# Expert layers: the layer norm's output added on VectorE and transposed onto the accumulators, in place of 32 products with the identity

## The chip, the cores and the metric

The kernel runs on one core of one Trainium2 chip. The metric is the time of one launch in microseconds (us), as the median of the runs. The engines of the core are named as the profile names them: PE is TensorE (PEld its weight loads, PEq and PEldq its queue), DVE is VectorE, ACT is ScalarE, POOL is GpSimd and SP is SyncE, which here starts the loads of the weights.

## What is computed

The reference takes 256 tokens of width 1024 through two blocks. The first has a feed-forward part, a mixer of attention and a recurrence, and a second feed-forward part. The second block has two layers, and each of them ends in the stage of this change: a layer norm, a mixture of 16 experts, and a term `ple` with a gate, summed before another layer norm.

```python
for i in range(DEPTH_2):
    ...
    x = layer_norm(DEEPNORM_ALPHA * x + mix, ln_mix_g[i], ln_mix_b[i])
    ple = (p[i] @ ple_w_proj[i]) * jax.nn.sigmoid(x @ ple_w_gate[i])
    ffn = grouped_moe(x, router_w, router_bias, moe_w1[i], moe_w3[i], moe_w2[i])
    x = layer_norm(DEEPNORM_ALPHA * x + ffn + ple, ln_ffn_g[i], ln_ffn_b[i])
```

`grouped_moe` picks two experts of a group for every token, and each expert computes `(silu(x @ w1) * (x @ w3)) @ w2`, weighted with the token's gate. The `x` on the last line is the layer norm's output itself; the change is about how this one summand comes into the sum.

## The kernel before

`moe_layer` emits one of the two expert layers. Eight pairs of experts, p = 0 to 7, run one after another in the loop at line 1397. The tokens that chose an expert are gathered into at most CAP slots by a product with one-hot columns (`gather`, tiles `xgp` in PSUM and `xg` in SBUF; `onehot` makes the columns `oh` on DVE). For each pair PE computes `h1` and `h3` (`up`, in the profile both called `h`), ACT and DVE make `es` of them (`hidden`), PE transposes it to `ehT` (`hidden_T`, line 1347), and `down` gives `ey`, two PSUM tiles for the two halves of the columns. ACT and DVE split `ey` into a rounded part `yh` and the rest `yl` (lines 332 and 335), and `combine` spreads both back over the tokens with the transposed one-hot columns `ohT`.

The loop is staggered. In the turn of pair p, PE starts `h1` of pair p + 1, transposes `es` of pair p, and goes on with `h1`; after `ey` of pair p comes `h3` of pair p + 1. I write h1(5) for the h1 of pair 5 and so on.

Up to pair 2, `combine` adds into SBUF tiles `acc` (the kernel's `x[t]`, one per half t of the tokens), since the gate's product holds the four PSUM accumulators. From pair 3 on, which is `last`, the accumulators are `comb`, two tiles of 512 columns for each half of the tokens, and the products add into them directly. At p == 3 the gated term `pg` is added onto `acc` on DVE (line 1424), and 32 products with the identity add the layer norm's output to `comb`: it lies transposed in SBUF as `xTh` (rounded) and `xTl` (the rest), eight chunks of 128 columns each, and a product with `identr` transposes a chunk back while it adds it. At p == 6 `acc` is split once more and added to `comb`, by 8 products with the identity.

```python
1437            if p == last:
1438                for t in range(2):
1439                    tk = slice(t * P, (t + 1) * P)
1440                    for k in range(8):
1441                        for t_ in (xTh, xTl):
1442                            mm(comb[t][k // 4][:, k % 4 * P:(k % 4 + 1) * P], t_[k][:, tk], identr,
1443                               start=False, stop=False, skip_group_check=True)
```

`mm` (line 342) is the helper that issues most products, so they bear line 343 in the profile.

At the start of p == 4, each engine loads `ci`, the largest number of tokens of an expert (line 1399), and branches on it (line 1400): if it exceeds CAP, `overflow` computes the surplus tokens, on all engines. With the inputs here the branch skips this code. On each engine some instructions of the turn of pair 3 come ahead of this branch and some behind it.

What sets the order: the code is written in the order of the source, and a scheduler then reorders each engine's instructions within a stretch without a branch, by the dependences and its own costs. The tiles come from pools with few slots, taken in turn: `Q` (SBUF, 512 columns, 9 slots), `PT` (PSUM, 4 slots), `PA` (PSUM, 4 slots, which the accumulators hold). A tile that takes the slot of an earlier one waits until that one has been read for the last time. SP streams the weights into rings of slots in SBUF.

## Time and profile before

| what | value |
|---|---|
| median of 3 runs | 1340.25 us (1339.31 to 1346.04) |
| span of the profiled execution, first to last instruction | 1338.8 us |
| PE busy | 1278.3 us, 95% of the span |
| DVE busy | 616.8 us, 46% |
| ACT busy | 521.4 us, 39% |
| expert layers' branch | at 794 us (first layer) and 1210 us (second) |

The profiled execution has no time of its own apart from its span, which lies 1.45 us below the median of the runs; what stands around the span, the launch and its end, is in that difference. The views used below are these. The timeline lists the work of an engine in order, with start and duration in us and, in brackets, the idle time ahead of it and what ended that; a row with "x16" holds 16 instructions in a row, and the duration of a product goes to the end of its last result, which overlaps with the start of the next row. A matmul of type f32 with 512 columns appears as two instructions. A view of a line lists the instructions of one source line, with the queue's own (TENSOR_LOAD, COMPARE_BRANCH, EVENT_SEMAPHORE) among them. Windows give the busy time of each engine in a stretch and PEclk, the granted clock of TensorE as a share of full speed.

### The profile page before, as it was taken

Reading aid. Unit: us, or ns where it says so; the run is one execution under the profiler, and the core shown is the slowest. Engines: PE = TensorE matmul, PEld = TensorE weight load, DVE = VectorE, ACT = ScalarE, POOL = GpSimd, SP = SyncE. Lnnn points to the kernel's source line nnn. Section 1 sums busy time; section 2 is a strip of 40 time slices with the busy share of each in tenths; the row PEclk is TensorE's granted clock in tenths of the full one; section 3 lists DMA queues with packets and bytes.
Section 4 is the critical chain, followed back from the end, with each engine's and each line's share of the span. In section 5 each row is a group of like instructions: output and inputs, shape, how many; then the busy total and the mean of one; then the engine's idle time right before and its main releaser. Section 6 shows DMA issues by size and latency. Waiting matters only on the chain. (4 is left out here: it accounts for less than half of the span.)

```text
span 1338.8 us, 19707 instructions
## 1 busy us (share of the span) xinstructions
PE 1278.3 (95%) x7758; PEld 908.3 (68%) x7758; DVE 616.8 (46%) x1021; ACT 521.4 (39%) x806; POOL 225.8 (17%) x224
## 2 busy tenths in 40 slices
PE   8999999999889999989999999997999999999996
PEld 7999997877879999878544554334988635454432
DVE  6544458796956476485341221107555522131113
ACT  5444445575445554335321131104686421131110
POOL 4000010002484263230011020004021110220001
PEclk9999999999999999999999999997999999998998
DMA  9766656444356556649899989998536698999990
GB/s 338 221 188 189 189 157 198 133 155 144 111 157 190 158 160 199 201 162 311 294 343 362 396 319 377 389 381 282 189 104 206 226 385 318 380 342 356 377 399 34
DMA packets 175277, 335.41 MB, mean 251 GB/s; under 512 B 10337, under 2 KB 72305, under 8 KB 175170
## 3 DMA queue, kind: packets, MB, share of 16 engines
q1 hardware_dynamic: 173696, 330.34, 71.2%
q0 software_dynamic: 896, 2.98, 0.6%
q8 instruction: 66, 1.08, 0.3%
q10 hardware_dynamic: 578, 0.67, 0.1%
q14 instruction: 41, 0.34, 0.1%
HBM read 332.91 MB, written 1.05 MB: 249 GB/s over the span
## 5 line engine op out<-in xcount | busy, mean ns | idle before, releaser
L316 DVE TENSOR_TENSOR wlo<-w,whi 128x1024 fp32r<-128x1024 f32 x200 | 254.5, 1278 | 201.7 <-ACT whi L301 197.8
L301 ACT ACTIVATE whi<-w 128x1024 fp32r<-128x1024 f32 x234 | 246.2, 1059 | 254.9 <-PE hT L339 107.2
L343 PE MATMUL h<-w,xg 128*64 128x512 f32 x1024 | 253.9, 606 | 0.0
L338 PE MATMUL hT<-xTh,whi 128*128 128x256 f32 x704 | 201.4, 286 | 3.1 <-ACT whi L301 3.0
L340 PE MATMUL hT<-xTh,wlo 128*128 128x256 f32 x704 | 200.5, 285 | 1.4 <-DVE wlo L316 1.4
L339 PE MATMUL hT<-xTl,whi 128*128 128x256 f32 x704 | 200.5, 285 | 0.2
L343 PEld LDWEIGHTS h<-w,xg 128*64 128x64 f32 x1024 | 73.3, 138 | 137.4 <-issue 128.1
L338 PEld LDWEIGHTS hT<-xTh,whi 128*128 128x128 f32 x704 | 136.5, 194 | 4.8 <-ACT whi L301 3.4
L340 PEld LDWEIGHTS hT<-xTh,wlo 128*128 128x128 f32 x704 | 136.2, 194 | 2.1 <-DVE wlo L316 2.0
L339 PEld LDWEIGHTS hT<-xTl,whi 128*128 128x128 f32 x704 | 136.2, 194 | 1.3 <-DVE xTl L334 0.8
L343 PE MATMUL ey<-w,ehTs 128*64 128x512 f32 x512 | 115.1, 595 | 0.2
L343 PEld LDWEIGHTS ey<-w,ehTs 128*64 128x64 f32 x512 | 38.3, 137 | 65.1 <-issue 60.8
L335 DVE SCALAR_TENSOR_TENSOR yl<-ey,sgate,yh 128x512 fp32r<-128x512 f32 x32 | 23.6, 749 | 124.2 <-ACT yh L332 123.4
L316 POOL TENSOR_TENSOR wlo<-w,whi 128x1024 fp32r<-128x1024 f32 x16 | 38.0, 2397 | 238.4 <-ACT whi L301 204.7
L338 PE MATMUL tr<-xTh,whi 128*128 128x256 f32 x256 | 73.6, 288 | 0.4 <-ACT xTh L332 0.4
L339 PE MATMUL tr<-xTl,whi 128*128 128x256 f32 x256 | 73.4, 287 | 0.3 <-DVE xTl L334 0.3
L340 PE MATMUL tr<-xTh,wlo 128*128 128x256 f32 x256 | 72.7, 284 | 0.4 <-DVE wlo L316 0.4
L339 PE MATMUL yacc<-wlo,hh 128*128 128x512 f32 x176 | 68.8, 391 | 2.0 <-DVE wlo L316 2.0
L1341 DVE TENSOR_TENSOR es<-es,h 128x512 f32<-128x512 f32 x16 | 11.0, 686 | 129.6 <-PE h L343 103.0
L338 PE MATMUL yacc<-whi,hh 128*128 128x512 f32 x176 | 68.8, 391 | 0.0
L340 PE MATMUL yacc<-whi,hl 128*128 128x512 f32 x176 | 68.6, 390 | 0.0
L332 ACT ACTIVATE yh<-ey,sgate 128x512 fp32r<-128x512 f32 x32 | 21.6, 687 | 113.8 <-PE ey L343 113.4
(444 smaller groups left out, 2142.7 us busy)
## 6 DMA issues: line engine op xcount, KB each, us to landing
w<-in_moe_w SPq DMA_DIRECT2D x384, 512.0 KB, 8.4
w<-in_ffn_w SPq DMA_DIRECT2D x132, 512.0 KB, 4.5
w<-in_w_in SPq DMA_DIRECT2D x28, 512.0 KB, 4.2
w<-in_sb_qkv SPq DMA_DIRECT2D x24, 512.0 KB, 10.3
w<-in_ple_gate SPq DMA_DIRECT2D x16, 512.0 KB, 8.0
w<-in_w_out SPq DMA_DIRECT2D x8, 512.0 KB, 3.4
w<-in_ab_w_in SPq DMA_DIRECT2D x8, 512.0 KB, 4.8
w<-in_ab_w_out SPq DMA_DIRECT2D x8, 512.0 KB, 3.6
```

The lines of the kernel that those rows point to most:

```text
L301: a = S.activation(hi, t, AF.Copy)
L316: i = eng.tensor_tensor(lo, t, fb(hi), op=OP.subtract)
L332: cur["act"] = S.activation(hi, src, AF.Copy if isinstance(scale, float) else AF.Identity, scale=scale)
L335: return V.scalar_tensor_tensor(lo, src, scale, fb(hi), op0=OP.mult, op1=OP.subtract)
L338: PE.matmul(o, lh, rh, start=start, stop=False)
L339: PE.matmul(o, lh, rl, start=False, stop=False)
L340: PE.matmul(o, ll, rh, start=False, stop=stop)
L343: PE.matmul(o, l, r, start=start, stop=stop, **kw)
L1341: V.tensor_tensor(s, s, h3, op=OP.mult)
```

## The change

The function that makes the transposed output now hands out the whole tiles too. At p == 3, after `combine`, four DVE adds sum the rounded part and the rest from SBUF into tiles `yT`, 16 PE transposes turn these into four PSUM tiles `yn`, and four DVE adds of 128x512 add `yn` onto `acc`. The identity products onto `comb` are gone; the 8 at p == 6, which add `acc`, are as before and now bring the layer norm's output too. Comments and some blank lines are also removed. The diff, cut to this:

```diff
@@ layer_norm_T: later
             split(0)
             split(1)
-            return chunks()
+            return chunks(), (hi, lo)
@@ moe_layer
             if p == 0:
-                xTh, xTl = xT()
+                (xTh, xTl), (whole_h, whole_l) = xT()
@@ moe_layer
             combine(p, y, o)
             if p == last:
+
+                yT = [Q([2, T], name="yT") for _ in range(4)]
+                for n in range(4):
+                    c = slice(n % 2 * 2, n % 2 * 2 + 2)
+                    V.tensor_tensor(yT[n], fb(whole_h[n // 2])[:, c], fb(whole_l[n // 2])[:, c], op=OP.add)
                 for t in range(2):
-                    tk = slice(t * P, (t + 1) * P)
-                    for k in range(8):
-                        for t_ in (xTh, xTl):
-                            mm(comb[t][k // 4][:, k % 4 * P:(k % 4 + 1) * P], t_[k][:, tk], identr,
-                               start=False, stop=False, skip_group_check=True)
+                    for kk in range(2):
+                        pn = PT([4, P], name="yn")
+                        for k in range(4):
+                            PE.transpose(pn[:, k, :], yT[2 * kk + k // 2][:, k % 2, t * P:(t + 1) * P], ident)
+                        d = slice(kk * 512, (kk + 1) * 512)
+                        V.tensor_tensor(x[t][:, d], x[t][:, d], pn.rearrange("p a b -> p (a b)"), op=OP.add)
             if p == 6:
```

Added lines shift the numbers of the lines behind; the branch keeps its lines 1399 and 1400.

The scheduler gives another order around the branch. On PE, in the first layer (the second is alike), this piece of the difference is the place right ahead of the branch; `comb` first twice for the first half of the tokens:

```order
 L343 MATMUL comb<-yh,ohT 128x512 x2
 L343 MATMUL comb<-yl,ohT 128x512 x2
+L343 MATMUL comb<-yh,ohT 128x512 x2
+L343 MATMUL comb<-yl,ohT 128x512 x2
+L1447 MATMUL yn<-identr,yT 128x128 x16
 L1399 TENSOR_LOAD ci
 L1400 COMPARE_AND_BRANCH
```

The four `comb` products of the second half and all 16 transposes now stand ahead of PE's load of `ci`. Behind the branch, at the place where its two paths meet, the difference is this (`h_9737` is h1(5)):

```order
 L1400 UNCONDITIONAL_BRANCH x2
-L343 MATMUL comb<-yh,ohT 128x512 x2
-L343 MATMUL comb<-yl,ohT 128x512 x2
-L343 MATMUL comb<-identr,xTh 128x128
-L343 MATMUL comb<-identr,xTl 128x128
...
 L343 MATMUL h_9737<-w_7530,xg 64x512
```

The four `comb` products and the 32 identity products are gone from here, and h1(5) follows the branch directly.

On DVE, ahead of the branch in the first layer, before (waits name the engine whose semaphore is awaited; `es_7705` is es of pair 4, `ci_6743` the count):

```order
L1424 TENSOR_TENSOR acc_7070<-acc_7070,pg_7660 128x512 [waits DVE_49]
L1424 TENSOR_TENSOR acc_7070<-acc_7070,pg_7664 128x512 [waits DVE_49]
L1341 TENSOR_TENSOR es_7705<-es_7705,h3_7672 128x512 [waits PE_49,Activation_49]
L1399 TENSOR_LOAD ci_6743 [waits DVE_49]
L1400 COMPARE_AND_BRANCH
```

and in the changed kernel:

```order
L1424 TENSOR_TENSOR acc_7070<-acc_7070,pg_7664 128x512 [waits DVE_49]
L1442 TENSOR_TENSOR yT_7716<-xTh_6982,xTl_6984 128x512 [waits DVE_49]
L1442 TENSOR_TENSOR yT_7717<-xTh_6982,xTl_6984 128x512 [waits DVE_49]
L1341 TENSOR_TENSOR es_7705<-es_7705,h3_7672 128x512 [waits PE_49,Activation_49]
L1442 TENSOR_TENSOR yT_7718<-xTh_6983,xTl_6985 128x512 [waits PE_49]
L1442 TENSOR_TENSOR yT_7719<-xTh_6983,xTl_6985 128x512 [waits PE_49]
L1449 TENSOR_TENSOR acc_7069<-acc_7069,yn_7724 128x512 [waits PE_49]
L1449 TENSOR_TENSOR acc_7069<-acc_7069,yn_7730 128x512 [waits PE_49]
L1449 TENSOR_TENSOR acc_7070<-acc_7070,yn_7736 128x512 [waits PE_49]
L1449 TENSOR_TENSOR acc_7070<-acc_7070,yn_7742 128x512 [waits PE_49]
L1399 TENSOR_LOAD ci_6743 [waits DVE_49]
L1400 COMPARE_AND_BRANCH
```

All eight adds stand ahead of the branch. `yT_7718` and `yT_7719` wait for PE: their slots are those of `yh` of pair 3, which `comb` of the second half reads last. The adds onto `acc` wait for the transposes. `yT_7716` and `yT_7717` stand ahead of `es`.

The third place is PE behind `ey` of pair 4, in the first layer; before (`h3_9829` is h3(5), `yh_9821` the first half of the columns of pair 4):

```order
L343 MATMUL ey_9788<-w323_7673,ehTs_9759 64x512
L343 MATMUL h3_9829<-w324_7675,xg_7444 64x512 [waits DMAHW2_49,DVE_49,Activation_49]
L343 MATMUL h3_9829<-w325_7681,xg_7444 64x512 [waits DMAHW3_49]
L343 MATMUL h3_9829<-w324_7675,xg_7444 64x512
L343 MATMUL h3_9829<-w325_7681,xg_7444 64x512
L343 MATMUL comb_7668<-yh_9821,ohT_9782 128x512 [waits Activation_49]
L343 MATMUL xgp_9870<-oh_9865,nh_6560 128x256 [waits DVE_49,PE_49]
```

and in the changed kernel:

```order
L343 MATMUL ey_9788<-w323_7673,ehTs_9759 64x512
L343 MATMUL comb_7668<-yh_9821,ohT_9782 128x512 [waits Activation_49]
L343 MATMUL comb_7670<-yh_9821,ohT_9782 128x512
L343 MATMUL h3_9829<-w324_7675,xg_7444 64x512 [waits DMAHW2_49,DVE_49,PE_49]
L343 MATMUL comb_7669<-yh_9823,ohT_9782 128x512 [waits Activation_49]
L343 MATMUL comb_7668<-yl_9822,ohT_9782 128x512 [waits DVE_49]
L343 MATMUL xgp_9870<-oh_9865,nh_6560 128x256 [waits DVE_49,PE_49]
```

`comb` on `yh` of pair 4 now follows `ey` directly, where four products of h3(5) stood between them. Further on, between the last product of h3(5) and the transposes of `es` of pair 5, there stood seven `comb` products and four of h1(6); now there are one of each.

## Rows read from the trace of the kernel before

**Rows 1.** The page: span, and busy time (share of the span) of the engines.

```profile
span 1338.8 us, 19707 instructions
...
PE 1278.3 (95%) x7758; PEld 908.3 (68%) x7758; DVE 616.8 (46%) x1021; ACT 521.4 (39%) x806; POOL 225.8 (17%) x224
```

**Rows 2.** Chain of work that ended last, first work behind the second branch: start us, us, what.

```profile
1213.36 7.37 PE comb L343 x36
```

**Rows 3.** Waits of PE, 1213 to 1330 us: us in total, times, longest us.

```profile
PE comb L343 <- PEq L1400: 2.0, 1, 2.0
PE comb L343 <- ACT yh L332: 1.6, 2, 0.8
PE ehT L1347 <- DVE es L1341: 0.9, 1, 0.9
```

**Rows 4.** Timeline of PE around the first branch: start us, us, engine, line, operation.

```profile
794.42 0.73 PE L343 MATMUL comb<-yh,ohT 128*128 128x512 f32 x2
...
797.70 0.70 PE L343 MATMUL comb<-yh,ohT 128*128 128x512 f32 x2 [2.08 <-PEq L1400]
...
798.81 0.31 PE L343 MATMUL comb<-identr,xTh 128*128 128x128 f32 x1
...
805.66 5.18 PE L343 MATMUL h<-w,xg 128*64 128x512 f32 x16
810.77 0.66 PE L1347 MATMUL ehT<-identr,es 128*128 128x128 f32 x4
811.36 3.65 PE L343 MATMUL h<-w,xg 128*64 128x512 f32 x16
```

**Rows 5.** Timeline of PE around the second branch.

```profile
1210.20 0.73 PE L343 MATMUL comb<-yh,ohT 128*128 128x512 f32 x2
...
1214.36 0.22 PE L343 MATMUL comb<-identr,xTh 128*128 128x128 f32 x1
...
1220.66 5.89 PE L343 MATMUL h<-w,xg 128*64 128x512 f32 x16
1226.48 0.66 PE L1347 MATMUL ehT<-identr,es 128*128 128x128 f32 x4
```

**Rows 6.** Line 1399, the load of ci: ns min/median/max, first and last start us.

```profile
L1399 PEldq TENSOR_LOAD <-ci x2: 315/400/485, 790.9 to 1206.7; - x2
```

**Rows 7.** Line 1400, the branch, in the queues of PE and DVE, same columns.

```profile
L1400 PEldq COMPARE_BRANCH  x2: 6032/6060/6087, 791.5 to 1207.1; - x2
L1400 DVEq COMPARE_BRANCH  x2: 72/72/72, 795.3 to 1210.9; - x2
...
L1400 DVEq EVENT_SEMAPHORE  x2: 21/21/21, 801.0 to 1211.4; - x2
```

**Rows 8.** Line 343, semaphore instructions in PE's queue.

```profile
L343 PEldq EVENT_SEMAPHORE  x68: 51/51/51, 412.2 to 1316.2; - x68
```

**Rows 9.** Line 1424, the adds of the gate onto the accumulators.

```profile
L1424 DVE TENSOR_TENSOR acc<-acc,pg x8: 684/686/689, 787.4 to 1206.2; 128x512 f32<-128x512 f32 x8
```

**Rows 10.** Timeline of PE at an earlier pause, in the mixer.

```profile
600.03 1.19 PE L343 MATMUL pool<-wsum,poolw 128*128 128x256 f32 x2 [4.07 <-DVE yg L994]
```

**Rows 11.** A window of 2 us behind the second branch: busy times, PEclk, DMA, GB/s.

```profile
1216.00:1218.00 2.00, 2.00 (x12) 2.00 (x11) 0.93 (x1) 0.00 (x0) 0.00 (x0) 0.50 1.05 386
```

**Rows 12.** Windows of 1 us after the earlier pause, same columns.

```profile
603.00:604.00 1.00, 1.00 (x4) 0.72 (x3) 0.81 (x2) 0.97 (x4) 0.00 (x0) 0.51 1.01 287
604.00:605.00 1.00, 1.00 (x6) 0.83 (x5) 0.42 (x1) 0.07 (x1) 0.00 (x0) 1.00 0.95 358
```

**Rows 13.** Timeline of PE behind ey of pair 4, first layer.

```profile
822.58 1.89 PE L343 MATMUL h<-w,xg 128*64 128x512 f32 x8
824.40 0.50 PE L343 MATMUL comb<-yh,ohT 128*128 128x512 f32 x1
```

**Rows 14.** Waits of PE's weight loads on a DMA, 797 to 912 us.

```profile
PEld h L343 <- DMA w<-in_moe_w: 0.9, 3, 0.4
```

**Rows 15.** Timeline of DVE behind ey of pair 4, first layer.

```profile
824.21 0.75 DVE L1168 TENSOR_TENSOR oh<-cst,rank 128x256 fp32r<-128x256 f32 x2
```

## Prediction

> **What bounds the kernel now.** I read the page first: PE is busy for 95% of the span, DVE for 46% [rows 1]. Then the chain that ended last: in the second expert layer it enters at the branch, its first piece of work is the 36 products that the change touches, and from there it is PE with few exceptions to the end [rows 2]. The waits of PE in that stretch show the exceptions: 2.0 us at the branch, 1.6 us for yh (two times), 0.9 us for es [rows 3]. No transfer is among them; even the weight loads, which run ahead, waited for a DMA 0.9 us in the largest group of the first expert layer [rows 14]. So a microsecond that PE loses or gains behind the branch should reach the end, in both layers. The place to cost is the stretch around the branch, in the timeline of PE [rows 4, 5].

> I call the start of the first comb product of pair 3 zero: 794.42 in the first layer, 1210.20 in the second. Before, h1(5), the first projection of pair 5, starts at +11.24 (805.66) and +10.46 (1220.66), and ehT(4), the transposes of pair 4, at +16.35 (810.77) and +16.28 (1226.48) [rows 4, 5]. The term for each layer is how these two move.

> **What goes.** The 32 identity products lie back to back on PE: 798.81 to 805.66 is 6.85 us in the first layer, 1214.36 to 1220.66 is 6.30 us in the second [rows 4, 5], 13.15 us together. [...] Ahead of it PE had stood idle for 2.08 us at the branch [rows 4].

> **What comes on VectorE.** Eight adds of 128x512 per layer. The nearest rows, eight adds of the same size, take 684 to 689 ns [rows 9]: 5.5 us, some 0.65 us from start to start when they follow each other. The two for yT0 and yT1 fit into the time in which DVE waits for h3; the other six don't. The order shows why: yT2 and yT3 take the slots of yh and so wait for comb of the second half of the tokens, and the four adds onto acc wait for the transposes.

> **What comes on PE, and what moves.** 16 transposes of 128x128. The four of ehT take 810.77 to 811.36, 0.59 us [rows 4], so 16 take 2.4 us at the high clock. The important thing is where they stand. Before, comb of the second half and the identity products stand behind the branch; now comb of the second half and the transposes stand ahead of it, and behind it stands h1(5) at once. So nothing is left that PE can do between the branch and h1(5).

> **The branch.** PE's sequencer spends 6.03 to 6.09 us in the compare-and-branch [rows 7]; with the load of ci ahead of it, from 790.9 [rows 6] to 797.70 [rows 4] is 6.8 us. Most of this is hidden before: the sequencer came to ci 3.5 us ahead of the first comb product (790.9 against 794.42), while PE still had queued products to run, and PE stood idle for 2.08 us only. After, the sequencer must first issue transposes that wait for DVE. That it stands still at such a wait is what I infer from a semaphore instruction of its queue: the last one is at 1316.2 [rows 8], just where the 0.9 us wait for es in [rows 3] ends, not ahead of it. So I take it that ci is reached only when yT3 is done.

> That moment, from zero: four comb products take 1.1 us (797.70 to 798.81 [rows 4]), eight 2.2 to 2.3. The yh products of the second half are the fifth and the sixth; they end at about +1.5 and +1.85 and set yT2 and yT3 free, which at 0.69 us each end at +2.2 and +2.9. I allow 0.3 us for the rest of the issue: ci at +3.2, 6.35 us or so later than before, and the first product behind the branch at 3.2 + 6.7 = **+9.9**.

> The second bound for h1(5) is DVE, for h1(5) also waits until DVE has passed the branch. Its last add onto acc starts at about +4.85, after 4 x 0.65 us from +2.9; ci and the branch end at +5.5. How long the passage takes, the trace tells two ways: in the first layer the semaphore behind the branch is at 801.0, 5.7 us after the branch at 795.3; in the second at 1211.4, 0.5 us after 1210.9 [rows 7]. I take each layer as it was: **+11.25** in the first, +6.0 in the second. The later of PE and DVE decides: h1(5) starts at +11.25 and +9.9.

> The rows thus show passages of some 6 us (PE twice, DVE once) and of 0.5 us (DVE once) [rows 7], and nothing in the trace binds the kind to the layer. [...]

> **The clock after the longer pause.** The transposes end at about +4.45, so PE now stands idle for 5.4 to 6.8 us, against 2.08. The nearest row with a long pause is 600.03: PE resumed after 4.07 us idle [rows 10] and the clock stayed low to 604.0, then rose to 1.00 [rows 12]. At half speed 3.97 us do the work of 1.99. The first half of h1(5), 16 products, is the size of the second half, 3.65 us at the high clock with the last product's tail [rows 4], some 3.55 without; so 3.55 + 2.0 = 5.55 us to ehT. Bounds: 3.55 (all high) and 7.1 (all low); the rows of before, 5.18 and 5.89 [rows 4, 5], lie between. ehT(4) starts at 11.25 + 5.55 = +16.8 in the first layer, +0.45 against before, and at 9.9 + 5.55 = +15.45 in the second, -0.8.

> **What moves behind ey(4).** Before, four products of h3(5) stand between ey(4) and comb of pair 4, 822.58 to 824.40 or 1.8 us, and cover the making of yh; PE has no idle time there [rows 13]. Now comb stands directly behind ey. Where PE waits for yh elsewhere, it is 0.8 us each time [rows 3]; I take 0.8, bounds 0 and 0.8. The gather xgp needs the one-hot columns, which DVE makes behind yl: 824.21 to 824.96 [rows 15], 1.6 to 2.4 us behind ey's end at 822.58, the first of them at 2.0. With yh 0.7 us later, that is 2.7; ahead of xgp now stand four comb products and one of h3, 1.1 + 0.45 us, behind the wait of 0.8, so PE comes there at about 2.3 and waits 0.4 (bounds 0 and 0.7). Between h3(5) and ehT(5) one comb and one h1 product are left, 0.7 us; es takes 0.9 us where nothing covers it [rows 3], so 0.2 remain (0 to 0.4). Sum +1.4 per layer (0 to 1.9), +2.8 in all. The comb products that no longer cover ehT(5) are not lost; they do their work earlier.

> **The sum.** +0.45 - 0.8 + 2.8 = +2.45 us. The profiled execution's span is 1338.8 [rows 1], 1.45 below the median of 1340.25; I add to the median: **1342.7 us**. 13.15 us of products go and nearly all of it comes back, as idle time at the branch (about 4 us more in each layer), as transposes and as uncovered waits. The runs of before reach from 1339.31 to 1346.04, and 0.5%, 6.7 us, is about what a measurement of this kernel can tell from no change.

> **The rivals.**
> 1. *The forecast, but DVE passes quickly in the first layer too.* Then h1(5) starts at +9.9 there as well: 1.35 us less, 1341.4. For it: DVE passed in 0.5 us in the second layer [rows 7]. Against: 5.7 us in this one.
> 2. *PE's sequencer runs ahead past the waiting transposes.* For it: it was 3.5 us ahead before. Against: [rows 8]. Then ci is reached at about zero, the branch ends at +6.7, and ehT starts at 6.7 + 5.55 = about +12.3 where DVE is quick: -4.0 in each layer, with +2.8 behind: 1335.0; with DVE slow in the first layer, +0.45 there, 1339.5.
> 3. *The plain gain.* The products go, and nothing takes their place: 1340.25 - 13.15 = 1327.1. Against: the order; no work of PE stands between the branch and h1(5).
> 4. *Slower, by DVE at the branch.* DVE takes 5.7 us in both layers, PE stands idle for 6.8 us, and the clock stays low through all of the first half of h1(5): ehT at 11.25 + 7.1 = +18.35, 2.0 and 2.1 later than before, and the waits behind ey at their upper ends, 2 x 1.9: +2.0 + 2.1 + 3.8 = +7.9, 1348.2. It decides as soon as the passage of DVE in the second layer exceeds 4.4 us (9.9 - 5.5). For it: 5.7 us in the first layer. Against: 0.5 us in the second.
> 5. *The change doesn't do what it says.* The order excludes it: the identity products are gone.

> **How the numbers follow.** Forecast 0.45, rival 1 0.22, rival 2 0.14, rival 3 0.04, rival 4 0.15. Predicted is the likeliest, 1342.7. Faster by over 0.5% (below 1333.5): rival 3 and a little of rival 2, 0.06. Slower by over 0.5% (above 1347): most of rival 4, 0.12. The rest, 0.82, is within. The range leaves out rival 3, a part of rival 2 and the upper half of rival 4: 1335 to 1348.

> **What would show it.** In the profile of the changed kernel: the load of ci on PE behind the start of comb, at about +3.2; PE's idle time ahead of h1(5) 5 to 7 us, put down to the branch; a granted clock of 0.50 for some us after it; the semaphore of DVE behind the branch 5.7 or 0.5 us after it; waits of comb for yh at pair 4. The forecast is wrong if PE's pause stays near 2 us (rival 2), if the clock is full at once (about 2 us less per layer), or if a wait on a DMA appears behind the branch, which would mean that the stream of weights, and not PE, sets the pace there.

## The result, and the profile after

The changed kernel is slower: a median of 1351.17 us (1347.02 to 1352.79) against 1341.15 us of before on the same chip, ratio 1.0055 with a 95% interval of [1.004, 1.007], which is +7.4 us (5.4 to 9.4). I had forecast 1342.7 us (+2.45 on the median of before), between 1335 and 1348. The sign of the sum was right and its size was not, and the time lies outside the range. The medians are 10.0 us apart, but a median of so few runs jumps, since the runs of before alone reach from 1339.31 to 1346.80; the ratio is worked out from all runs. Differences below go by the ratio unless the text names the medians or the timelines.

The page of after: the span, and busy time of the engines (share of the span), to be laid beside [rows 1].

```profile
span 1349.4 us, 19658 instructions
...
PE 1277.1 (95%) x7726; PEld 902.8 (67%) x7726; DVE 625.1 (46%) x1037; ACT 520.5 (39%) x806; POOL 226.1 (17%) x224
```

32 identity products per layer are gone, yet PE's busy time falls by 1.2 us only, and the span is 10.6 us longer. The waits of PE from 785 us to the end, after (us in total, times, longest us):

```profile
PE h L343 <- PEq L1400: 12.0, 2, 6.1
PE comb L343 <- ACT yh L332: 5.6, 7, 0.8
```

The lines of the same view of before that stand against these:

```profile
PE comb L343 <- PEq L1400: 4.0, 2, 2.1
PE comb L343 <- ACT yh L332: 3.2, 4, 0.8
```

The wait at the branch has tripled, and it is now `h` that waits, not `comb`. The wait for yh has grown too. The timeline of PE around the two branches, after (start us, us, engine, line, operation, count, idle time ahead and what ended it):

```profile
797.84 0.73 PE L343 MATMUL comb<-yh,ohT 128*128 128x512 f32 x2
...
799.79 2.17 PE L1447 MATMUL yn<-identr,yT 128*128 128x128 f32 x16
808.09 5.29 PE L343 MATMUL h<-w,xg 128*64 128x512 f32 x10 [6.12 <-PEq L1400]
813.63 1.93 PE L343 MATMUL h<-w,xg 128*64 128x512 f32 x6 [0.25 <-issue]
815.49 0.66 PE L1347 MATMUL ehT<-identr,es 128*128 128x128 f32 x4
...
1218.01 0.73 PE L343 MATMUL comb<-yh,ohT 128*128 128x512 f32 x2
...
1219.96 2.17 PE L1447 MATMUL yn<-identr,yT 128*128 128x128 f32 x16
1227.97 6.14 PE L343 MATMUL h<-w,xg 128*64 128x512 f32 x16 [5.84 <-PEq L1400]
1234.04 0.66 PE L1347 MATMUL ehT<-identr,es 128*128 128x128 f32 x4
...
1238.93 7.14 PE L343 MATMUL ey<-w,ehTs 128*64 128x512 f32 x32
1246.83 0.73 PE L343 MATMUL comb<-yh,ohT 128*128 128x512 f32 x2 [0.76 <-DMA w<-in_moe_w]
```

Zero, the first comb product of pair 3, is now 797.84 and 1218.01. From it h1(5) starts at +10.25 and +9.96 and ehT(4) at +17.65 and +16.03. Before, ehT(4) stood at +16.35 and +16.28 [rows 4, 5], so the stretch around the branch costs 1.30 us in the first layer and gains 0.25 in the second. The rest is lost behind it. From ehT(4) to the first comb product of pair 4 is 12.79 us in the second layer of after (1234.04 to 1246.83).

In numbers, from the timelines of both kernels: from ehT(4) to the end of ey(4) 12.03 us (before 11.81) in either layer; from there to the first comb product of pair 5, 36.85 and 36.86 us (before 33.97 both times). That is 0.22 + 2.88 = 3.10 us per layer. (For before, the end of ey(4) is where h3(5) starts beside its last results, 822.58.) With the border, 1.30 - 0.25 + 2 x 3.10 = 7.25 us, which is the +7.4 of the ratio. The profiled execution lost 3.4 us more, all ahead of the first instruction that the change touches: zero of the first layer lies at 797.84 against 794.42, with the same instructions before it. Single executions differ by that much: in the traces of all the kernels here zero of the first layer lies between 792.54 (e6) and 798.75 (e4). So I leave it out, and compare kernels below also by the timelines, from zero to the first comb product of pair 7, both layers together. That stretch is 230.6 us in before and 237.9 in after.

The queues at the branch in after: PE's load of ci, then the branch on PE and DVE and the semaphore of DVE behind it (ns min/median/max, first and last start us), to be laid beside [rows 6, 7].

```profile
L1399 PEldq TENSOR_LOAD <-ci x2: 315/405/495, 800.7 to 1220.9; - x2
...
L1400 PEldq COMPARE_BRANCH  x2: 6209/6250/6292, 801.3 to 1221.3; - x2
L1400 DVEq COMPARE_BRANCH  x2: 72/72/72, 802.6 to 1222.6; - x2
L1400 DVEq EVENT_SEMAPHORE  x2: 21/21/21, 803.9 to 1223.2; - x2
```

PE reaches ci at +2.86 and +2.89, where before it was there 3.5 us ahead of zero. It spends 6.2 to 6.3 us in the branch. DVE passes in 1.3 and 0.6 us, quickly in both layers. The granted clock (PEclk, the number behind the five engines' busy times) in 1 us windows of after:

```profile
812.00:813.00 1.00, 1.00 (x2) 0.00 (x0) 0.00 (x0) 0.00 (x0) 0.00 (x0) 0.50 0.35 109
...
814.00:815.00 1.00, 1.00 (x6) 0.27 (x2) 0.00 (x0) 0.00 (x0) 0.00 (x0) 1.00 0.96 360
...
1232.00:1233.00 1.00, 1.00 (x4) 0.26 (x2) 0.00 (x0) 0.00 (x0) 0.00 (x0) 0.50 0.61 109
1233.00:1234.00 1.00, 1.00 (x6) 0.15 (x2) 0.00 (x0) 0.00 (x0) 0.00 (x0) 0.99 0.61 201
```

After the pause of 6 us PE works at a granted clock of 0.50, the level of [rows 11], for about 5 us (808.09 to 813, 1227.97 to 1233), longer than the 3.97 us of [rows 12].

Behind ey(4), first layer, after, the rows in which PE waits or goes on with h3(5):

```profile
828.28 0.74 PE L343 MATMUL comb<-yh,ohT 128*128 128x512 f32 x2 [0.76 <-ACT yh L332]
828.95 1.07 PE L343 MATMUL h<-w,xg 128*64 128x512 f32 x2
829.95 0.50 PE L343 MATMUL comb<-yh,ohT 128*128 128x512 f32 x1
...
830.96 1.93 PE L343 MATMUL h<-w,xg 128*64 128x512 f32 x6
832.82 0.39 PE L343 MATMUL xgp<-oh,nh 128*128 128x256 f32 x1
...
856.47 7.09 PE L343 MATMUL ey<-w,ehTs 128*64 128x512 f32 x32
864.37 0.73 PE L343 MATMUL comb<-yh,ohT 128*128 128x512 f32 x2 [0.81 <-ACT yh L332]
```

Here is what the forecast had not seen. Products of `h` and `ey` have tiles of 64 columns (128*64), and the records show two of them running side by side: each appears as two rows, and 8 rows, four products, take 1.82 us from start to start in [rows 13] (822.58 to 824.40). A group of one product (x2) and a group of three (x6) together hold the same four, but take 1.00 us (828.95 to 829.95) and 1.86 (830.96 to 832.82), 2.86 in all. A product without a partner, here, took as long as two. I call a group boundary after an odd number of products a torn pair. There are five of these between ey(4) and ey(5) in each layer of after. Before had three, and one more that drew in ey(5). The timeline of PE of before shows it, and that two products do run at once: the last product of h1(6) starts beside one of ey(5), 0.01 us apart.

```profile
849.07 0.59 PE L343 MATMUL h<-w,xg 128*64 128x512 f32 x1
849.08 7.45 PE L343 MATMUL ey<-w,ehTs 128*64 128x512 f32 x31
```

### The profile page after: what moved, and what is told of

The parts are those of the page before. It is cut to its first block, busy times and chain, and to the rows that moved or that the text cites. A ratio compares the mean times of both kernels' runs of the same rounds, so it can differ in the third digit from the quotient of the medians.

```text
span 1349.4 us, 19658 instructions
## 1 busy us (share of the span) xinstructions
PE 1277.1 (95%) x7726; PEld 902.8 (67%) x7726; DVE 625.1 (46%) x1037; ACT 520.5 (39%) x806; POOL 226.1 (17%) x224
## 3 DMA queue, kind: packets, MB, share of 16 engines
HBM read 332.91 MB, written 1.05 MB: 247 GB/s over the span
## 5 line engine op out<-in xcount | busy, mean ns | idle before, releaser
L343 PE MATMUL h<-w,xg 128*64 128x512 f32 x1024 | 258.4, 608 | 12.2 <-PEq L1400 12.0
```

Source lines behind the costliest of these rows:

```text
L343: PE.matmul(o, l, r, start=start, stop=stop, **kw)
```

## The experiments

PE's order is what the experiments change. For it, every product and transpose of PE from h1(5) to comb of pair 5 is noted in the order of the source (0 to 39 h1(5) with ehT(4), the score products and ey(4); 40 to 55 h3(5); 56 to 87 the gather; 88 to 95 comb of pair 4; 96 to 103 and 108 to 115 h1(6); 104 to 107 ehT(5); 116 to 119 the score products; 120 to 135 ey(5); 136 to 151 h3(6); 152 to 159 comb of pair 5), and then chained in the order that a list gives:

```diff
-        PE.matmul(o, l, r, start=start, stop=stop, **kw)
+        cur.setdefault('log', []).append(PE.matmul(o, l, r, start=start, stop=stop, **kw))
...
-            combine(p, y, o)
+            combine(p, y, o); p == 5 and [after(cur['log'][b], cur['log'][a]) for a, b in zip(PE_ORDER, PE_ORDER[1:])]
```

The theory that these rows suggest (A): the border is worth about +1 us in all, and the loss is the order of PE behind ey(4). The rival (B): the pause at the branch with the clock behind it is the loss.

**The changed kernel with the order of before behind the branch** (e1_after_border), and **the kernel before with the order of after** (e2_before_aorder). Only the list differs; e1 is the changed kernel, e2 the kernel before. The part of the lists behind ey(4):

```diff
+e1: PE_ORDER = [..., 40, 41, 42, 43, 88, 56, 57, 44, 58, 59, 60, 61, 62, 63, 45, 46, 47, 64, ...]
+e2: PE_ORDER = [..., 88, 92, 40, 89, 90, 56, 57, 64, 41, 42, 43, 58, 59, 60, 61, 62, 44, 63, ...]
```

> The changed kernel, with PE's instructions of pairs 4 and 5 behind the branch held in the order that they have in the kernel before; all other engines keep the order of the changed kernel. Theory A: nearly all of the loss sits behind ey of pair 4, in PE's new order (waits for yh of pair 4, 0.76 us, and of pair 5, 0.81 us, and pairs of h products torn apart by other products, some 1.5 us; 3.1 us per layer), and the branch with its pause is worth only +1.3 us in the first layer and -0.25 us in the second. Then this kernel loses 6.1 us against the changed one and stands 1 us above the kernel before, ratio about 1.001. Rival B: the loss comes from the longer pause at the branch and the low clock behind it, and the order is worth at most the 2.8 us of the prediction: then it stays 4 us or more above the kernel before, ratio 1.003 or more.

> The kernel before, identity products and all, with PE's instructions of pairs 4 and 5 behind the branch held in the order that they have in the changed kernel; nothing else differs. Theory A: the order alone costs 6.1 us, 1341 + 6 = 1347 us, ratio 1.0045, and the profile shows the waits for yh at pairs 4 and 5, which this kernel without the order does not have. Rival B: 2.8 us or less, ratio 1.002 or less.

Measured: e1 1343.22 us against 1341.64, ratio 1.0014 [0.9994, 1.0033]; e2 1349.79 us, ratio 1.0048 [1.0028, 1.0067]. The waits of PE, e1, 785 us to the end:

```profile
PE h L343 <- PEq L1400: 12.0, 2, 6.2
...
PE comb L343 <- ACT yh L332: 3.2, 4, 0.8
```

And e2:

```profile
PE comb L343 <- ACT yh L332: 6.4, 8, 0.8
...
PE comb L343 <- PEq L1400: 4.3, 2, 2.3
```

e1 keeps the whole pause at the branch, 12.0 us, and is not to be told from before; its interval just reaches B's 1.003. e2 keeps the identity products and the short pause and has the loss, with an interval wholly above B's 1.002. The timelines are sharper: the stretch is 231.9 us in e1 and 237.1 in e2, against 230.6 and 237.9. So A: nearly all of the time was lost behind ey(4), by the order that the scheduler chose there. The kernel before can have that order too, so it does not hang on where the layer norm's output is added.

**Pairs made whole in the kernel before** (e4_before_pairs): in three places of h3(5) per layer, one and three products become two and two.

```diff
-PE_ORDER = [..., 57, 44, 58, 59, 60, 61, 62, 63, 45, 46, 47, 64, ...]
+PE_ORDER = [..., 57, 44, 45, 58, 59, 60, 61, 62, 63, 46, 47, 64, ...]
```

> The kernel before, with one thing changed in PE's order: in three places of h3 of pair 5 in each layer the gather's products stand behind both experts' products of a chunk instead of between them (1 | 3 becomes 2 | 2; as many groups as before). Theory C: the products of the two experts of a pair fill one half of PE's columns each and run side by side, so a group of one product takes as long as a group of two (the rows of 2 instructions take 1.00 us, those of 6 take 1.86 us, those of 8 take 1.82 us), and a torn pair costs 0.86 us: 3 x 0.86 = 2.6 us per layer, 5.2 us in all are gained, 1336 us, ratio 0.996, with rows of 4 instructions at 1.0 us. Rival D: what costs is the change between kinds of products, some 0.55 us a time whichever way they are grouped; then the time stays at 1341 us, ratio 1.000.

Measured: 1339.57 us, ratio 0.9965 [0.9948, 0.9982], 4.7 us less (5.1 by the timelines): 0.78 us for each of the six. Timeline of PE, e4, the first of the new groups:

```profile
829.53 1.08 PE L343 MATMUL h<-w,xg 128*64 128x512 f32 x4
```

A group of two products (x4) takes as long as a group of one (1.07 us in after at 828.95). So C holds: 2.86 us for one and three become 2 x 1.01 for two and two, a torn pair is 0.84 by the rows, and an interruption without tearing costs 2.02 - 1.82 = 0.20.

**Pairs made whole in the changed kernel** (e9_after_pairs), the direct test on the kernel in question, in its five places per layer; and **cover for yh besides** (e10_after_cover): four products of h3(5) ahead of comb of pair 4, four of h3(6) ahead of comb of pair 5. The first line is the changed kernel's own order.

```diff
-own:   PE_ORDER = [..., 88, 92, 40, 89, 90, 56, 57, 64, 41, 42, 43, 58, 59, 60, 61, 62, 44, 63, ...]
+e9:    PE_ORDER = [..., 88, 92, 40, 41, 89, 90, 56, 57, 64, 42, 43, 58, 59, 60, 61, 62, 44, 45, 63, ...]
+e10:   PE_ORDER = [..., 40, 41, 42, 43, 88, 92, 89, 90, 56, 57, 64, 58, 59, 60, 61, 62, 44, 45, 63, ...]
```

> The changed kernel with its own order, but in five places of each expert layer where a group of one product of h and a group of three follow each other with other products between them, the order is now two and two (h3(5) four times, h1(6) once). Nothing else moves; the waits for yh stay. The changed kernel stood at 1.0055 of before. Theory C (products of 64 columns run two at a time, and a group with an odd number costs what the earlier run showed, 4.7 us for six places, 0.78 each): 10 x 0.78 = 7.8 us less, ratio to before 1.0055 - 0.0058 = 0.9997, between 0.998 and 1.0015. Theory D (the loss behind ey comes only from the waits for yh and the border; the grouping costs nothing here): the ratio stays at 1.0035 or above.

> As the run with two and two, and besides four products of h3(5) stand ahead of comb of pair 4, and four of the next projection ahead of comb of pair 5, as cover for the making of yh. Theory W (the two waits for yh, 0.76 and 0.81 us, are real losses of the changed order): both go, 2 x 1.57 = 3.1 us; a torn pair at comb of pair 5 goes too, 2 x 0.78 = 1.6, and one interruption of h, about 0.26 each: together about 5.3 us less than the run with two and two, ratio about 0.9957, between 0.994 and 0.9975. Theory X (the time comes back at the next wait, of xgp for oh or ehT for es): not more than 2 us less, ratio 0.998 or above, with the new wait in the list of waits.

Measured: e9 1340.70 us against 1342.66, ratio 0.9994 [0.9977, 1.0012]. Against the changed kernel's 1.0055, which comes from another set of runs, that is 0.0061 or 8.2 us less, 0.82 us for each of the ten. The timelines agree: from comb of pair 4 to comb of pair 5 it is 36.09 us in after and 31.86 in e9, 4.23 us for the five of a layer. e10 1335.72 us, ratio 0.9949 [0.9933, 0.9965], another 6.0 us (5.0 by the medians). Timeline of PE, e9, first layer:

```profile
827.04 0.73 PE L343 MATMUL comb<-yh,ohT 128*128 128x512 f32 x2 [0.77 <-DMA w<-in_moe_w]
827.70 1.08 PE L343 MATMUL h<-w,xg 128*64 128x512 f32 x4
...
858.90 0.73 PE L343 MATMUL comb<-yh,ohT 128*128 128x512 f32 x2 [0.81 <-ACT yh L332]
```

The same places in e10:

```profile
823.05 1.94 PE L343 MATMUL h<-w,xg 128*64 128x512 f32 x8
824.92 0.96 PE L343 MATMUL comb<-yh,ohT 128*128 128x512 f32 x3
...
853.37 1.94 PE L343 MATMUL h<-w,xg 128*64 128x512 f32 x8
855.24 0.96 PE L343 MATMUL comb<-yh,ohT 128*128 128x512 f32 x3
```

Both came out on the side of C and W. W's 5.3 us lies near the runs; by the timelines, from ehT(4) to comb of pair 7, e10 gains 3.9 us per layer, 1.3 more than W counted, and where that comes from I did not find. In e10 the two waits for yh are gone, and no new wait stands in the list: its waits for oh (2.7 us) and es (1.7 us) are those of after. (At 827.04 of e9 and 1246.83 of after the row names a weight transfer. The comb product reads no weights, and in after the two yh of ACT run from 1246.09 to 1247.35, so that the first is done at about 1246.8, when the product starts. I take it for the same wait.) e10 has the change, the pause at the branch (6.39 us in the first layer) and the slow first half of h1(5) behind it (7.50 us) in it, and still beats before by 0.5%.

**The removal alone** (e3_noident_border): the kernel before without the identity products, in the order of before. The layer norm's output is left out of the sum.

```diff
-            if p == last:
-                for t in range(2):
...
-                            mm(comb[t][k // 4][:, k % 4 * P:(k % 4 + 1) * P], t_[k][:, tk], identr,
```

> The kernel before without the 32 identity products of each layer and with nothing in their place (the layer norm's output is left out of the sum), PE's order of pairs 4 and 5 as in the kernel before. This measures what the products themselves are worth. If they are worth their place in the timeline, 13.15 us go: 1328 us, ratio 0.990. If the pause at the branch takes a part back (h1 of pair 5 must wait until DVE has passed the branch, and the clock is low behind the pause for 4 us of PE's work or more): comb ends at +4.4 us, h1 starts at +4.4 to +6.6 instead of +11.2 and +10.5 and its first half takes 5.5 to 7 us, so 9 to 12 us go: 1329 to 1332 us, ratio 0.991 to 0.993.

Measured: 1332.44 us, ratio 0.9927 [0.9902, 0.9952], 9.8 us less, not the 13.15 us that the products took. Timeline of PE, e3, the first layer:

```profile
801.48 5.77 PE L343 MATMUL h<-w,xg 128*64 128x512 f32 x16 [1.99 <-DVEq L1400]
```

With the products gone h1(5) waits 2.0 us for DVE behind the branch, in the first layer only. From zero to ehT(4) it gains 3.9 us there and 6.8 in the second, where the products took 6.85 and 6.30. So in the first layer the identity products had covered a part of the branch, which was the premise of the forecast, and in the second their whole time is won; rival 3, the plain gain, was not to be had whole.

**PE in the order of the source** for the whole stretch from h1(5) to comb of pair 6: the kernel before (e5_before_source), the changed one (e6_after_source), the changed one with the sums, transposes and adds moved into the turn of pair 4 behind the second half of h1(5) (e7_late_source), and the changed one without load of ci, branch and overflow code (e8_after_nobranch).

```diff
e5, e6, e7, e8:
-            combine(p, y, o)
+            combine(p, y, o); p == 6 and [after(b, a) for a, b in zip(cur['log'], cur['log'][1:])]
e7, the block of the change:
-            if p == last:
+            if p == 4:
e8:
-                v = nc.values_load(ci[0:1, 0:1], min_val=0, max_val=T)
-                with tc.If(v > CAP):
-                    overflow(i, x, nh, nl, late, row)
```

> The kernel before, with PE's instructions behind the branch, from h1 of pair 5 to comb of pair 6, held in the order of the source: h3 whole, then the gather, then comb. Theory C (the two experts' products run side by side, and a torn pair costs 0.86 to 1.04 us): the kernel before has eight torn pairs per layer there (three in h3 of pair 5, one in h1 of pair 6, one in h3 of pair 6, three in h3 of pair 7) and waits 0.8 us for yh of pair 6; all of this goes: 8 x 0.95 + 0.8 = 8.4 us per layer, 16.8 us in all, 1325 us, ratio 0.9875. Rival E: the stream of weights, whose DMA share is about 1 in this stretch, can't follow, and half of it or more comes back as waits on a DMA: ratio 0.994 or more.

> The changed kernel with PE held in the same order of the source as its sister without the change. This tells what the change is worth when the order behind the branch is no longer part of it. From the stretches around the branch (+1.3 us in the first layer, -0.25 us in the second) it should stand 1 us above that sister: 1326 us, ratio 0.988. Rival B (the pause and the low clock are the loss): 4 us or more above it, ratio 0.9905 or more.

> The idea of the change at another place, with PE in the order of the source: the sum on VectorE, the 16 transposes and the adds onto the accumulators are emitted at pair 4 behind h1 of pair 5, where PE's clock is high again, and comb of the second half of the tokens stays behind the branch. The pause at the branch should then be the 2 us of the kernel before, not 6. The products gone are worth 9.8 us in two layers (measured without them), the transposes cost 16 at 0.14 us, 2.2 us per layer: 5.4 us less than the kernel before with the same order, 1319.5 us, ratio 0.984. Rival: DVE comes late with the sums, since it passes the branch only at 6 to 11 us behind comb, and PE waits for them: 1325 us or more, ratio 0.9875 or more.

> The changed kernel in the order of the source, without the branch on the count and without the code for surplus tokens behind it (the load of the count and the overflow are left out). It prices the branch: if the pause and the low clock after it come from the branch, h1 of pair 5 follows the transposes at once, 5.9 and 5.6 us earlier, and its first half takes 3.6 us instead of 7.4 and 6.1: 9.6 + 8.1 = 17.7 us less than the changed kernel with the branch in the same order, 1308 us, ratio 0.975. Rival: the clock falls in any case at this place, or PE waits for VectorE's sums and adds: 6 us or more of it stay.

Measured, against 1342.37 us of before in the same runs:

| kernel | median us | ratio | interval |
|---|---|---|---|
| e5, before in source order | 1313.55 | 0.9776 | [0.9746, 0.9806] |
| e6, after in source order | 1314.29 | 0.9794 | [0.9768, 0.982] |
| e7, moved behind h1(5) | 1305.49 | 0.9729 | [0.9705, 0.9753] |
| e8, after without the branch | 1293.75 | 0.9642 | [0.9617, 0.9666] |

e5 gained nearly twice what was expected. The expectation had counted torn pairs and not the many interruptions between whole ones. With the prices above the three turns of the first layer come to 9 torn pairs (9 x 0.84 = 7.6), some 14 interruptions (2.8) and two waits, for yh and es, that go (1.7): 12.1 us of the 14.5 us per layer that the timelines show. The rest I did not find. Timeline of PE, e5: h3(5) as one group.

```profile
822.09 7.04 PE L343 MATMUL h<-w,xg 128*64 128x512 f32 x32
```

e6 differs from e5 by the change alone, at the same order behind the branch: +0.7 us by the medians, +2.4 by the ratios, and the intervals overlap. Six runs of each can't tell that from B's 4 us, but the timelines can: the stretch is 201.5 us in e5 and 202.1 in e6, +0.6. So with the order taken out the change gains nothing here, much as the border terms had said (1.30 - 0.25 = +1.05). e7 shows what would have to be done for it to be worth something. Timeline of PE, e7, both branches:

```profile
798.27 0.71 PE L343 MATMUL comb<-yh,ohT 128*128 128x512 f32 x2 [2.26 <-PEq L1400]
...
801.49 5.81 PE L343 MATMUL h<-w,xg 128*64 128x512 f32 x16 [1.82 <-DMA w<-in_moe_w]
...
811.40 2.09 PE L1417 MATMUL yn<-identr,yT 128*128 128x128 f32 x16
...
1196.45 0.71 PE L343 MATMUL comb<-yh,ohT 128*128 128x512 f32 x2 [1.98 <-PEq L1400]
...
1197.56 3.65 PE L343 MATMUL h<-w,xg 128*64 128x512 f32 x16
```

Here nothing new waits for DVE ahead of the branch, and the pause that PE's queue ends there is 2.26 and 1.98 us, as short as before. (The 1.82 us at 801.49 are put down to a weight transfer. But in e3 the wait at this place ends at 801.48 and names DVE, whose semaphore behind the branch is at 801.2. I take it for the same wait.) In the second layer the first half of h1(5) takes 3.65 us from its start, as long as the second half in before, where the granted clock was 1.00 (811.36, windows of 810 to 814). e7 is the fastest kernel of the study that does all the work, 2.7% below before; of that, by the medians, 28.8 us are the order (e5) and 8.1 us the change in its new place, where 5.4 had been expected. By the timelines it is 29.1 and 8.0. e8 bounds the branch. Timeline of PE, e8, first layer:

```profile
800.33 2.17 PE L1447 MATMUL yn<-identr,yT 128*128 128x128 f32 x16
802.43 3.65 PE L343 MATMUL h<-w,xg 128*64 128x512 f32 x16
```

Without the branch h1(5) follows the transposes at once, its first half in the same 3.65 us, and the two layers save 20.5 us against e6. By the timelines of both, h1(5) starts 6.1 us sooner after the transposes in each layer, and its first half is 3.5 us shorter in the first layer and 2.3 us in the second (3.58 us to ehT(4), where e6 took 7.12 and 5.86): 18.0 us. From ehT(4) to comb of pair 7 the two timelines are the same, 84.4 us in each layer. The remaining 2.5 us of the medians lie within the spread of these runs (e6 alone reaches from 1306.86 to 1317.89).

## Why the prediction was wrong

**What bounds the kernel: right.** What PE lost or gained behind the branch reached the end: by the timelines +7.3 us in after, -29.1 in e5 and -8.0 from e5 to e7, by the runs +7.4, -28.8 and -8.1. No wait on a transfer took its place in after or in e10.

**What goes: right,** and 13.15 us of products went for nothing. e3 shows that 9.8 us of it could be had (10.7 by the timelines). The changed kernel gives that back at the border: against e3 its h1(5) starts 3.5 and 5.5 us later from zero, behind the transposes and the longer pause, and the first half of h1(5) takes 1.7 and 1.0 us longer.

**The queue and the branch: right.** ci at +2.86 against +3.2, the branch 6.25 us against 6.06, h1(5) at +9.96 in the second layer against +9.9. yT2 and yT3, which free the transposes, ran from 799.31 to 800.60, that is to +2.76, and ci came 0.1 us later, in the second layer as well: PE's sequencer stood still at the transposes that waited for DVE. Rival 2 is out. (The forecast's "6.35 us or so later than before" should have been 6.7, from 3.5 us ahead of zero to +3.2; +9.9 does not use it. Measured it is 6.4.) The compare-and-branch took 72 ns on DVE in both kernels, and on PE 6.0 to 6.1 us before and 6.2 to 6.3 us in after.

**DVE at the branch: wrong, and it mattered little.** I kept the 5.7 us of the first layer; DVE passed in 1.3 us. So PE alone decided, h1(5) came at +10.25 and not at +11.25, and rival 1's condition held while its price was eaten by the next step. Rival 4, the slower case, rested on the opposite. It was wrong as a mechanism, and that its time, 1348.2, is the nearest of all is luck.

**The clock after the pause: mis-sized.** I took 5.55 us from h1(5) to ehT(4), with 3.97 us of slow clock. The granted clock was 0.50 for about 5 us, and the step took 6.07 us in the second layer. In the first it took 7.40 us: h1(5) stopped after five products (x10) for 0.25 us, put down to issue, and the next group is torn. That stop stands in the first layer of e1, e6, e9 and e10 as well (0.76, 0.52, 0.29 and 0.94 us), and in none of the kernels without the long pause. What it is I did not find out. Together with the line above: ehT(4) moved by +1.30 and -0.25, where the forecast had +0.45 and -0.8; 1.4 us of the miss.

**Behind ey(4): the step that failed.** It was to cost 1.4 us per layer, and it cost 3.10. Of its terms the wait for yh of pair 4 was right in size (0.8 forecast, 0.76 measured), the waits of xgp for oh (0.4) and of ehT for es (0.2) did not come. The reason for the first was seen only in part, as ey(4) of PE and yh of ACT show, three rows of before (the last at pair 5) and one of after:

```profile
815.66 7.09 PE L343 MATMUL ey<-w,ehTs 128*64 128x512 f32 x32
821.97 0.69 ACT L332 ACTIVATE yh<-ey,sgate 128x512 fp32r<-128x512 f32 x1 [5.82 <-PE ey L343]
855.81 1.45 ACT L332 ACTIVATE yh<-ey,sgate 128x512 fp32r<-128x512 f32 x2 [11.03 <-PE ey L343]
...
827.54 1.27 ACT L332 ACTIVATE yh<-ey,sgate 128x512 fp32r<-128x512 f32 x2 [6.68 <-PE ey L343]
```

Before, ACT started the first yh of pair 4 while the last products of ey(4) still ran, at 821.97 against their end at 822.75. In after it starts both at 827.54, when ey(4) has ended. The new order had also changed the last eight products of ey(4) (32, 34, 33, 35, 36, 38, 37, 39 in the list of e2, 32 to 39 in turn in e1), so that both halves are complete together. With the earlier order the first yh would have been done at 822.66, and comb directly behind ey(4) would hardly have waited for it; that is an estimate, and no run tested it. Three terms were missing:
- a wait for yh of pair 5, 0.81 us. Before, the last product of ey(5) ran without a partner, and yh of the first half was made beside it, from 855.81.
- one torn pair more (five against four), 0.84 us.
- two more interruptions of h (11 groups of h between ey(4) and ey(5) against 10, and comb between ey and h), 0.20 each.

Their sum with the first term is 0.76 + 0.81 + 0.84 + 0.40 = 2.81 of 2.88 us. The 0.22 us ahead of it are the tail of ey(4): it starts 4.89 us behind ehT(4) in both kernels, but before, h3(5) started 6.92 us later, beside the last results of ey(4), and in after the wait begins only when these are out, 7.14 us later. e9 took out all five torn pairs, and e10 the two waits besides, and the time went the way of the sum; the price of an interruption was not tested by itself.

The mistake in method: I costed the order behind ey(4) by its waits alone, as if a product cost the same in whatever order. The rows for it were there in the trace of before: x2 in 1.00 us, x6 in 1.86 us and x8 in 1.82 us, start to start. And the bounds, 0 to 1.9 per layer, were worked out from those waits, so the range was too narrow upward; it left out even rival 4's own 1348.2. With 3.1 in place of 1.4 and the rest as forecast, the sum is 1346.1, and with the border as measured it is 1347.5, both still inside the range. Of the 3.7 us from there to 1351.17, 0.9 are the higher median of before in these runs, and the rest is what the medians show beyond the timelines. So this step accounts for 3.4 us of the miss and the border for 1.4; that the time fell outside the range is in part the spread of the runs.

## What to carry to other kernels

When an edit makes a scheduler choose another order, cost the order itself: lay the groups of before and after side by side, and look for rows of the same work whose time depends on how it is grouped (here 1.00 + 1.86 us against 1.82). Ahead of a branch, do not put work that makes an engine's queue wait for another engine: here PE's queue came to ci 6.4 us later, and of the 6.0 to 6.3 us that the branch takes on PE in both kernels, the pause that is left open grew from 2.1 and 2.0 us to 6.1 and 5.8. And where an edit shows nothing or a small loss, separate its own effect from the order that came with it, by fixing the order in both kernels; here the first was about +0.6 us by the timelines and the second about +6.
